# Second to fourth expert's down tiles freed singly, one load of each expert's count, and a first gather by token halves, in a one-core transformer layer

## The chip, the cores and the metric

The kernel is one layer of a diffusion backbone on one core of one Trainium2 chip. The metric is the device time of one execution in microseconds (us), the median of the runs shown. The core has a matrix engine (TensorE, PE), three engines for elementwise work (VectorE = DVE, ScalarE = ACT, GpSimd = POOL), and a sequencer without arithmetic (SyncE, SP) that issues here almost all transfers from memory (HBM) into the on-chip buffer (SBUF). PE writes to the accumulators (PSUM).

## The reference

For 256 latent tokens of width 1024 (plus 256 context tokens) the layer computes a mixer (gated linear attention and latent attention, merged and projected) and then a mixture of experts. Only the second part matters here:

```python
def _moe(h, p):
    tok = h.reshape(-1, d)
    logits = (tok @ p["router_w"] + p["router_b"]).astype(jnp.float32)
    top_v, top_i = lax.top_k(logits, TOP_K)          # 4 of 32
    wts = jax.nn.softmax(top_v, axis=-1)
    combine = jnp.sum(jax.nn.one_hot(top_i, N_EXPERTS) * wts[..., None], axis=1)
    out = jnp.zeros_like(tok)
    for e in range(N_EXPERTS):
        gate = jnp.minimum(tok @ p["w_gate"][e] + p["b_gate"][e], SWIGLU_LIMIT)
        up = jnp.clip(tok @ p["w_up"][e] + p["b_up"][e], -SWIGLU_LIMIT, SWIGLU_LIMIT)
        act = (up + 1.0) * gate * jax.nn.sigmoid(SWIGLU_ALPHA * gate)
        out = out + combine[:, e:e + 1] * (act @ p["w_down"][e] + p["b_down"][e])
    return out.reshape(b, t_len, d)
```

All weights are float32: 32 experts with three 1024 x 1024 matrices are 384 MiB, read once.

## The kernel before, in words

**Weights.** Each expert's three matrices come as six tiles of 2 MiB, in the order gate, gate, up, up, down, down (the last two experts have their downs at the very end). The tiles are called w0, w1, ... here, in the order of their issue: w0 to w5 are the first expert's, w6 to w11 the second's, and so on. `Ring` holds ten places: tile w(i) may be issued only when w(i-10) has been used and its place was given back with `ring.done` (line 92), which calls `pump`, whose transfers are issued on SP (L77). SP runs its list in order, so a transfer that waits for its place holds up everything behind it.

**One expert.** An expert has up to 64 token slots in the main path. The tokens of two experts at a time are gathered (`select` makes one-hot columns G on DVE from the position table `posm`, `gather` multiplies them with x1 on PE into `p_xg`, in two halves g of four 128-column blocks, and DVE and ACT scale the blocks into X). Then `project` for gate and up (PE, into `p_gate` and `p_up`), `gated` and `upped` (DVE, ACT), `turn` (four transposes on PE into `p_aT`, copied by ACT to aT), `down` (PE into `p_y`), `halves` (ACT, DVE), and `scatter`, which adds the result into the accumulators `acc`. The scatter of an expert is done in the next expert's turn. `slot_tokens` (PE `p_st`, then DVE) makes the slot-to-token table.

**Overflow.** An expert with more than 64 tokens has a second path inside `tc.If(rv > 0)`; rv is a register loaded from `trips` by `blocks(e)` (L1554), on every engine. In this run only the first expert of those looked at here takes that path; the others branch over it. A further block, `crowded()` (L1502, after the expert with index 20), is for still fuller experts and is branched over as well.

**When places are freed.** The first expert (index 0) and those with index 1 to 3 (`e < SINGLE`) give back each gate and up tile by itself with `freed(1)`; the first expert does so with its downs too, the next three give both downs back at once with `ring.done(2)` behind the whole down product. Experts with index 4 to 9 free in pairs. `freed` loads rv anew, ordered behind the transfer that it issued.

**Order on the engines.** In this part PE runs in the order in which the code is written (`manual_schedule` for PE). SP, DVE and ACT are ordered by the scheduler, so where register loads and branches stand on SP does not follow from the source alone.

**Before the experts.** The router's choice for the two halves of 128 tokens (`best`, `choose`), the positions (`p_pos`, `posm`), and the gather of the first two experts stand between the mixer and the first product. `more_gather` gathers the overflow tokens of the first expert; its `p_xg` takes a PSUM place of the same two-place tag as the main gather's.

Of the kernel before, what the change touches and what calls it, by code (L numbers as in the profile page):

```python
# [8 lines left out]
F32 = mybir.dt.float32  # L9
# [10 lines left out]
NE = 32  # L20
SLOTS = 64
# [108 lines left out]
def block_kernel(ctx: ExitStack, tc: tile.TileContext, a, out):  # L130
# [71 lines left out]
    def mm(o, l, r, start, stop):  # L202
        nc.tensor.matmul(o, l, r, start=start, stop=stop)  # L203
# [18 lines left out]
    def bank(name, shape=(128, 512)):  # L222
        return ps.tile(list(shape), F32, tag="b", bufs=3, name=name)
# [928 lines left out]
    def softmax(t, step):  # L1152

        v = sm[t]
        if step == 0:
            nc.vector.tensor_scalar(v[:, 4:5], mx[:, t, 0:1], -1.0, None, op0=ALU.mult)
            nc.scalar.activation(v[:, 0:4], mx[:, t, 0:4], AF.Exp, bias=v[:, 4:5], accum_out=v[:, 5:6])
        else:
            nc.vector.reciprocal(v[:, 6:7], v[:, 5:6])
            nc.vector.tensor_scalar(v[:, 0:4], v[:, 0:4], v[:, 6:7], None, op0=ALU.mult)  # L1160
            nc.vector.tensor_mul(eq[t], eq[t], v[:, 0:4].unsqueeze(1).to_broadcast([128, 32, 4]))
            nc.vector.tensor_reduce(comb[:, t], eq[t], axis=mybir.AxisListType.X, op=ALU.add)

# [67 lines left out]
    def best(t, p):  # L1231
        lg = lgs[t]
        nc.vector.scalar_tensor_tensor(lg, p, r2[t], rb, op0=ALU.mult, op1=ALU.add)
        nc.vector.max(mx[:, t], lg)
        nc.vector.max_index(ix[:, t], mx[:, t], lg)
        nc.vector.tensor_scalar(ixf[:, t], ix[:, t, :4], 1.0, None, op0=ALU.add)

    def choose(t):

        nc.vector.tensor_tensor(eq[t], iota[:, :32].unsqueeze(2).to_broadcast([128, 32, 4]),  # L1240
                                ixf[:, t].unsqueeze(1).to_broadcast([128, 32, 4]), op=ALU.is_equal)
        with nc.allow_low_precision(reason="0 or 1"):
            nc.vector.tensor_reduce(maskb[:, t], eq[t], axis=mybir.AxisListType.X, op=ALU.add)
# [5 lines left out]
    def warm(n):  # L1249

        for _ in range(n):
            mm(pw, zero.to_broadcast([128, 128]), zero.to_broadcast([128, 512]), True, True)
# [28 lines left out]
    p1 = logits(1)  # L1281
    choose(0)
    softmax(0, 0)
    best(1, p1)
    choose(1)
    softmax(1, 0)
    close(psz_cm)
    pa_cm, psa = pool("ps_acc", space=PSUM, reuse_waits="tile")
    acc = [[psa.tile([128, 512], F32, tag=f"acc{t}{n}", name=f"acc{t}{n}") for n in range(2)] for t in range(2)]
    for t in range(2):  # L1290
        for n in range(2):
            mm(acc[t][n], zero.to_broadcast([128, 128]), zero.to_broadcast([128, 512]), True, False)
    warm(4)
    p = bank("p_pos", (128, 3, 32))
    mm(p[:, 0], ltb, maskb[:, 0], True, True)
    mm(p[:, 1], ltb, maskb[:, 1], True, False)
    mm(p[:, 1], oneb, maskb[:, 0], False, True)
    mm(p[:, 2], oneb, maskb[:, 0], True, False)
    mm(p[:, 2], oneb, maskb[:, 1], False, True)
    nc.vector.scalar_tensor_tensor(posm, p[:, 0:2], 1.0, maskb, op0=ALU.add, op1=ALU.mult)  # L1300
    count = late.tile([1, 32], F32, name="count")
    trips = late.tile([1, 40], I32, name="trips")
    nc.scalar.copy(count, p[0:1, 2])

    close(ps_cm)
    pb_cm, psb = pool("ps_moe", space=PSUM, side="right", reuse_waits="tile")

    def bankb(name, shape=(128, 512), tag="b"):
        return psb.tile(list(shape), F32, tag=tag, bufs=2, name=name)

    close(op_cm)
    close(pre_cm)
# [11 lines left out]
    ring.pump()  # L1324
    loaded = ring.last

    def select(G, i, e):

        for t in range(2):
            nc.vector.tensor_scalar(G[:, t, i], iota[:, :SLOTS], posm[:, t, e:e + 1], r2[t], op0=ALU.is_equal, op1=ALU.mult)  # L1330

    def gather(X, G, g):

        p = bankb("p_xg", (128, 4, SLOTS * EB))
        for k in range(4):
            for t in range(2):
                mm(p[:, k], x1[:, t, ts(4 * g + k, 128)], G[:, t], t == 0, t == 1)
        for k in range(4):
            j = 4 * g + k
            if k % 2:  # L1340
                nc.scalar.activation(X[:, j], p[:, k], AF.Identity, bias=fB[:, 0, j:j + 1], scale=fA[:, 0, j:j + 1])
            else:
                nc.vector.tensor_scalar(X[:, j], p[:, k], fA[:, 0, j:j + 1], fB[:, 0, j:j + 1],  # L1343
                                        op0=ALU.mult, op1=ALU.add)
# [18 lines left out]
    def slot_tokens(of, sid, tag=""):  # L1363

        p = bankb("p_st")
        mm(p, of.to_broadcast([128, 128]), where, True, True)
        n = 1 if tag else 2
        S = mo.tile([128, 2, 128], F32R, tag="S" + tag, bufs=2, name="S")
        w = mo.tile([128, 1], F32, tag="wt" + tag, bufs=n, name="wt")
        hit = mo.tile([128, 256], BF16, tag="hit", name="hit")  # L1370
        s = S.rearrange("p a b -> p (a b)")
        nc.vector.tensor_scalar(s, p[:, :256], sid, None, op0=ALU.is_equal)
        nc.vector.scalar_tensor_tensor(hit, s.bitcast(F32), 1.0, p[:, 256:], op0=ALU.mult, op1=ALU.mult, accum_out=w)
        return S, w

    def block_tiles():
        return (mo.tile([128, 2, EB, SLOTS], F32, tag="G", name="G"),
                mo.tile([128, 8, EB * SLOTS], F32, tag="X", bufs=2, name="X"))
# [69 lines left out]
    def turn(u, slots, tag="", aT=None):  # L1448
        nt = slots // 16
        p = bankb("p_aT", (128, nt, 128), tag="b" if tag else "g")  # L1450
        for k in range(nt):
            nc.tensor.transpose(p[:, k], u[:, ts(k, 128)], C("ident"))  # L1452
        if aT is None:
            aT = mo.tile([128, nt, 128], F32, tag="aT" + tag, name="aT")
        nc.scalar.copy(aT, p)  # L1455
        return aT
# [24 lines left out]
    def scatter(S, ys):  # L1481

        for t in range(2):
            for y in ys:
                for h in range(2):
                    r = slice(SLOTS * h, SLOTS * h + SLOTS)
                    mm(acc[t][h], S[r, t], y[r], False, False)
# [41 lines left out]

    todo, gtf = None, bd  # L1530
    G, X = block_tiles()
    for i in range(EB):
        select(G, i, i)
    more = more_gather(SLOTS, posm[:, :, 0:1])
    next(more)
    gather(X, G, 0)
    gather(X, G, 1)
    next(more)
    next(more)

# [9 lines left out]
    def blocks(e, ins=None):  # L1550
        with ExitStack() as es:
            if ins is not None:
                es.enter_context(tc.issue_after(ins))
            return nc.values_load(trips[:1, e:e + 1], min_val=0, max_val=(256 - SLOTS) // MORE)  # L1554
# [10 lines left out]
            return Ws[4 + n][:, k]  # L1565
        return Ws[4 + k // 4][:, k % 4, ts(n, 512)]

    ends = {}
    for e in range(NE):
        i = e % EB  # L1570
        if e and i == 0:
            X = Xn
        Ws = [ring.take() for _ in range(6 if e < NE - 2 else 4)]

        def W(c, j):
# [8 lines left out]
        def freed(n):  # L1584

            ring.done(n)
            return blocks(e, ring.last.ins)

        if e == 0:

# [80 lines left out]
                else:  # L1671
                    ring.done(4)
        following = list(range(e - i + EB, e - i + 2 * EB))
        if following[0] < NE:
            if i == 0:
                Gn, Xn = block_tiles()
                for k, f in enumerate(following):
                    select(Gn, k, f)
                gather(Xn, Gn, 0)
            if i == 1:  # L1680
                gather(Xn, Gn, 1)
        aT = turn(u, SLOTS, aT=aT_last if e == NE - 1 else None)
        if e == NE - 1:
            pass
        elif e:
            scatter(*todo)
        if e + 1 < NE:
            toks[e + 1] = slot_tokens(sel[:, e + 1:e + 2], first_sid)
        if e == 24:

            cbT = mo.tile([128, 2, 128], F32, tag="aT1", name="cbT")
# [8 lines left out]
            row_all(gtf, 1, bankb)  # L1700
        S = toks.pop(e)[0]

        if e == 0:
            p = bankb("p_y", tag="g")
            ps_ = [bankb(f"p_y1{n}") for n in range(2)]
            for half in range(2):
                ks = range(4 * half, 4 * half + 4)
                down(aT, lambda k: Ws[4 + k // 4][:, k % 4], p, ks)
                if half:
                    todo = S, halves(p)  # L1710
                with tc.If(rv > 0):
                    if half == 0:
                        a1T = turn(u1, MORE, "1")
                    for n in range(2):
                        down_parts(a1T, lambda k: w_of(e, k, n), MORE, ps_[n], ks)
                    if half:
                        more_out(S1, ps_)
                rv = freed(1)
        elif e < NE - 2:
            todo = S, halves(down(aT, lambda k: Ws[4 + k // 4][:, k % 4], bankb("p_y", tag="g")))  # L1720
            with tc.If(rv > 0):  # L1721
                a1T = turn(u1, MORE, "1")
                more_out(S1, [down_parts(a1T, lambda k: w_of(e, k, n), MORE, bankb(f"p_y1{n}")) for n in range(2)])
            ring.done(2)
        else:
            ends[e] = S, S1, aT, u1, rv
# [181 lines left out]
```

## Time and profile before

| | |
|---|---|
| time, median of 3 runs (lowest, highest) | 1249.0 us (1248.04, 1249.89) |
| time of the profiled execution; its span | 1249.03 us; 1247.3 us |
| TensorE's granted clock, mean | 0.986 of full speed |
| PE busy, share of the span | 1147.7 us, 92% |
| DVE, ACT, POOL busy | 403.2, 243.9, 78.4 us |
| read from HBM | 460.53 MB, 370 GB/s over the span |

The span goes from the first to the last instruction in the trace. PE's busy share counts matmuls that are pipelined and whose ends are modelled, so 92% does not say that PE sets the time; the transfer rate by slices, below, has to be read beside it.

### The profile page before, as it was taken

The numbers are of one execution on the slowest core, as the hardware profiler recorded it, in microseconds if no ns is written. First come the engines' busy times: TensorE is split into PE (matmuls) and PEld (weight loads), VectorE is DVE, ScalarE is ACT, GpSimd is POOL, SyncE is SP. The second block draws the span as 40 slices with busy tenths as digits, with TensorE's granted clock in tenths as the row PEclk, the third lists the DMA queues.
The fourth block names the chain that finished last, engine by engine and source line by source line (L and its number), as shares of the span: only waits on it lengthen the run. The fifth ranks groups of instructions, "written<-read, shape, count | busy, mean of one in ns | idle before, by whom it ended". The sixth has DMA issues, their size and how long they took to land. (4 is left out here: it accounts for less than half of the span.)

```text
span 1247.3 us, 16381 instructions
## 1 busy us (share of the span) xinstructions
PE 1147.7 (92%) x6494; PEld 610.3 (49%) x6495; DVE 403.2 (32%) x780; ACT 243.9 (20%) x425; POOL 78.4 (6%) x61
## 2 busy tenths in 40 slices
PE   8999999999998999999999899999879989999886
PEld 5776699885333344444444344444334434444332
DVE  5667686675211212212121221222112211111112
ACT  4565544443200000101010010101000100101001
POOL 2355101300000000000000000000000000000000
PEclk9999999999999999999999999999989999999999
DMA  8933446986889999999999999999899999999995
GB/s 350 352 142 138 189 171 256 387 349 272 304 346 424 422 427 426 426 426 424 428 425 426 426 427 427 425 424 426 374 376 425 427 427 426 425 427 424 426 426 218
DMA packets 37190, 463.52 MB, mean 372 GB/s; under 512 B 4504, under 2 KB 4760, under 8 KB 9280
## 3 DMA queue, kind: packets, MB, share of 16 engines
q1 hardware_dynamic: 36336, 460.90, 88.7%
q8 instruction: 101, 1.65, 0.5%
q10 hardware_dynamic: 720, 0.70, 0.2%
q14 instruction: 33, 0.27, 0.1%
HBM read 460.53 MB, written 1.05 MB: 370 GB/s over the span
## 5 line engine op out<-in xcount | busy, mean ns | idle before, releaser
L203 PE MATMUL p_up<-w,X 128*64 128x512 f32 x1024 | 228.9, 594 | 10.5 <-DMA w<-in_w_up_dram 7.6
L203 PE MATMUL p_gate<-w,X 128*64 128x512 f32 x1024 | 229.9, 597 | 3.9 <-DMA w<-in_w_gate_dram 2.1
L203 PE MATMUL p_y<-w,aT 128*64 128x512 f32 (+1 forms) x1056 | 230.1, 601 | 1.8 <-ACT aT L1455 1.4
L203 PEld LDWEIGHTS p_up<-w,X 128*64 128x64 f32 x1024 | 91.4, 137 | 132.0 <-issue 113.5
L203 PEld LDWEIGHTS p_gate<-w,X 128*64 128x64 f32 x1024 | 94.1, 138 | 116.5 <-issue 113.5
L203 PEld LDWEIGHTS p_y<-w,aT 128*64 128x64 f32 (+1 forms) x1056 | 70.5, 136 | 141.6 <-issue 137.3
L1420 DVE TENSOR_SCALAR g<-p_gate 128x512 f32<-128x512 f32 x32 | 22.1, 692 | 221.8 <-PE p_gate L203 212.6
L203 PE MATMUL p_xg<-G,x 128*128 128x128 f32 x512 | 70.7, 295 | 24.3 <-PEq L1664 18.9
L1478 DVE TENSOR_TENSOR yl<-p_y,yh 128x512 fp32r<-128x512 f32 x31 | 21.4, 691 | 218.2 <-ACT yh L1477 209.2
L203 PEld LDWEIGHTS p_xg<-G,x 128*128 128x128 f32 x512 | 65.1, 206 | 49.3 <-issue 49.3
L1455 ACT COPY aT<-p_aT 128x512 f32<-128x512 f32 (+1 forms) x33 | 18.9, 574 | 309.8 <-PE p_aT L1452 309.8
L1425 DVE TENSOR_SCALAR u<-p_up 128x512 f32<-128x512 f32 x32 | 22.1, 691 | 170.6 <-PE p_up L203 170.6
L1421 ACT ACTIVATE s<-g 128x512 f32<-128x512 f32 (+1 forms) x34 | 21.0, 618 | 281.4 <-DVE g L1420 281.4
L1190 POOL TENSOR_TENSOR rx<-rx,cst 128x1 f32<-128x1 f32 x4 | 2.7, 674 | 992.3 <-DVE rx L1189 992.3
L1477 ACT CAST yh<-p_y 128x512 fp32r<-128x512 f32 x31 | 18.2, 586 | 205.9 <-PEq L1721 186.7
L203 PEld LDWEIGHTS <-selb 128*64 128x64 bf16 (+2 forms) x178 | 15.8, 104 | 80.7 <-issue 78.9
L1343 DVE TENSOR_SCALAR X<-p_xg,mA_gpref,mB_gpref 128x128 f32<-128x128 f32 x64 | 26.2, 409 | 69.2 <-PE p_xg L203 49.3
L203 PE MATMUL p_gate<-h0h,wsl 128*128 128x256 f32 x160 | 45.5, 284 | 2.5 <-DVE wsl L370 2.5
L203 PE MATMUL p_gate<-h0h,wsh 128*128 128x256 f32 x160 | 46.7, 292 | 0.0
L203 PE MATMUL p_gate<-h0l,wsh 128*128 128x256 f32 x160 | 44.9, 280 | 0.0
L370 DVE TENSOR_TENSOR wsl<-p,wsh 128x1024 fp32r<-128x1024 f32 x27 | 35.4, 1310 | 11.6 <-ACT wsh L369 11.5
L328 POOL TENSOR_TENSOR sums<-sums,f 128x1024 f32<-128x1024 f32 x14 | 35.8, 2590 | 33.5 <-ACT f L326 22.2
(422 smaller groups left out, 1392.6 us busy)
## 6 DMA issues: line engine op xcount, KB each, us to landing
w<-in_w_up_dram SPq DMA_DIRECT2D x64, 2048.0 KB, 31.2
w<-in_w_gate_dram SPq DMA_DIRECT2D x64, 2048.0 KB, 30.8
w<-in_w_down_dram SPq DMA_DIRECT2D x62, 2048.0 KB, 25.8
p<-in_w_in_dram SPq DMA_DIRECT2D x7, 2048.0 KB, 9.5
a<-in_w_mod_a_dram SPq DMA_DIRECT2D x8, 1024.0 KB, 9.6
f<-in_w_mod_f_dram SPq DMA_DIRECT2D x4, 2048.0 KB, 8.6
g<-in_w_mod_g_dram SPq DMA_DIRECT2D x4, 2048.0 KB, 8.4
wo<-in_w_out_dram SPq DMA_DIRECT2D x2, 2048.0 KB, 15.3
```

What stands on the lines that cost most here:

```text
L203: nc.tensor.matmul(o, l, r, start=start, stop=stop)
L328: nc.gpsimd.tensor_add(to, to, v)
L370: (eng or nc.vector).tensor_sub(lo, src, hi.bitcast(F32))
L1190: nc.gpsimd.tensor_tensor(dst, dst, C("nhalf")[:, :1], op=ALU.pow)
L1343: nc.vector.tensor_scalar(X[:, j], p[:, k], fA[:, 0, j:j + 1], fB[:, 0, j:j + 1], op0=ALU.mult, op1=ALU.add)
L1420: nc.vector.tensor_scalar(g, pg, LIMIT, None, op0=ALU.min)
L1421: nc.scalar.activation(s, g, AF.Sigmoid, scale=ALPHA)
L1425: nc.vector.tensor_scalar(u, pu, LIMIT, -LIMIT, op0=ALU.min, op1=ALU.max)
L1455: nc.scalar.copy(aT, p)
L1477: nc.scalar.copy(hi, p)
L1478: nc.vector.tensor_sub(lo, p, hi.bitcast(F32))
```

## The change: what it does

1. **Head.** The second half's choice (`best`, `choose`, `softmax` for tokens 128 to 255) is written behind the product that gives the first half's positions; `posm` is made for each half by itself. Six zero products (`warm`) stand between the two position products. The first gather runs by token halves: all eight blocks for the first 128 tokens, then all eight for the others, into two banks at once.
2. **First expert.** The gather of the next pair moves behind the downs; the next expert's `slot_tokens` ahead of the turn.
3. **Second to fourth expert** (index 1 to 3). The scatter of the expert before moves ahead of the turn, the gather behind the downs, and the downs are done and freed in two halves, each with its own `If`.
4. **Count.** `freed` returns the rv that the expert already has and loads nothing.

```diff
-    best(1, p1)
-    choose(1)
-    softmax(1, 0)
...
+    mm(p[:, 0], ltb, maskb[:, 0], True, True)
+    warm(6)
+    best(1, p1)
+    choose(1)
+    place_of(0)
+    softmax(1, 0)
+    mm(p[:, 1], oneb, maskb[:, 0], True, False)
+    mm(p[:, 1], ltb, maskb[:, 1], False, True)
...
+    pg = [bankb(f"p_xg{g}", (128, 4, SLOTS * EB)) for g in range(2)]
+    for t in range(2):
+        for i in range(EB):
+            select(G, i, i, [t])
+        if t == 0:
+            place_of(1)
+            nc.scalar.copy(count, p[0:1, 2])
+        for g in range(2):
+            for k in range(4):
+                mm(pg[g][:, k], x1[:, t, ts(4 * g + k, 128)], G[:, t], t == 0 and k == 0, t == 1 and k == 3)
...
             ring.done(n)
-            return blocks(e, ring.last.ins)
+            return rv
...
+        select_next()
+        if not single:
+            for_next()
         elif e:
             scatter(*todo)
-        if e + 1 < NE:
-            toks[e + 1] = slot_tokens(sel[:, e + 1:e + 2], first_sid)
+        else:
+            tokens_next()
+        aT = turn(u, SLOTS, aT=aT_last if e == NE - 1 else None)
+        if not single and e < NE - 1:
+            scatter(*todo)
+        if e:
+            tokens_next()
...
-        if e == 0:
+        if single:
             p = bankb("p_y", tag="g")
             ps_ = [bankb(f"p_y1{n}") for n in range(2)]
             for half in range(2):
...
                 rv = freed(1)
+            for_next()
```

`for_next` is the gather of the next pair, `tokens_next` is `slot_tokens` for the next expert.

**PE, second expert, from the end of its up product to the next expert.** w_2984 and w_3047 are its two down tiles (w10 and w11) in the kernel before. There it reads, without the rows inside the `If` that repeat:

```order
L1644 UNCONDITIONAL_BRANCH x2
L1554 TENSOR_LOAD trips
L203 MATMUL p_xg<-G,x_2294 128x128 x8
L1452 MATMUL p_aT<-cst,u 128x128 x4
L203 MATMUL acc_2811<-yh,S 128x512
...
L203 MATMUL p_st<-where,selb 128x512
L203 MATMUL p_y<-w_2984,aT 64x512 x8
L203 MATMUL p_y<-w_3047,aT 64x512 x8
L1721 COMPARE_AND_BRANCH
...
L1721 UNCONDITIONAL_BRANCH x2
```

In the changed kernel the same two tiles are w_2988 and w_3037:

```order
L1659 UNCONDITIONAL_BRANCH x2
L203 MATMUL acc_2803<-yh,S 128x512
...
L1458 MATMUL p_aT<-cst,u 128x128 x4
L203 LDWEIGHTS selb
L203 MATMUL p_st<-where,selb 128x512
L203 MATMUL p_y<-w_2988,aT 64x512 x8
L1740 COMPARE_AND_BRANCH
...
L203 MATMUL p_y<-w_3037,aT 64x512 x8
L1740 COMPARE_AND_BRANCH
...
L1740 UNCONDITIONAL_BRANCH x2
L203 MATMUL p_xg<-G,x_2294 128x128 x8
```

The register load and the gather are gone from in front of the transposes, the scatter stands there, the downs are parted by a branch, and the gather follows them.

**SP, around the branch over `crowded()`.** In the kernel before, w_8879 is w126 and w_8881 is w127; nothing stands between the end of that branch and w127:

```order
L77 DMA w_8877<-in_w_down_dram 128x4096
L77 DMA w_8879<-in_w_gate_dram 128x4096
L1721 COMPARE_AND_BRANCH
L1721 UNCONDITIONAL_BRANCH x2
L1502 COMPARE_AND_BRANCH
...
L1502 UNCONDITIONAL_BRANCH
L77 DMA w_8881<-in_w_gate_dram 128x4096
```

In the changed kernel w_8852 is w135 and w_9297 is w136. The pair of rows TENSOR_LOAD and ISA x2 of L1569 stands eleven times in a row, of which one is shown:

```order
L77 DMA w_8850<-in_w_up_dram 128x4096
L77 DMA w_8852<-in_w_up_dram 128x4096
L1758 TENSOR_LOAD trips
L1508 COMPARE_AND_BRANCH
...
L1508 UNCONDITIONAL_BRANCH
L1758 ISA x2
L1569 TENSOR_LOAD trips
L1569 ISA x2
...
L1679 COMPARE_AND_BRANCH
L1679 UNCONDITIONAL_BRANCH x2
L77 DMA w_9297<-in_w_down_dram 128x4096
```

The branch over `crowded()` has moved nine tiles further down SP's list, and the counts of the eleven experts that follow (index 21 to 31) are now loaded on SP between that branch and the next transfer. In the kernel before such bunches of loads (nine, twelve, twelve and three) stand ahead of w11, w20, w26 and w32.

**PE, ahead of the first expert.** p_xg is the gather; w_2199 is the first gate tile. Before, from the last position product on:

```order
L203 MATMUL p_pos<-maskb,oneb 128x32
L203 MATMUL p_xg<-G,x_2294 128x128 x16
L203 MATMUL p_xg<-x_2294,G 32x256 x8
L203 LDWEIGHTS selb
L203 MATMUL p_gate<-RB,selb 64x512
```

In the changed kernel p_xg_2868 and p_xg_2869 are the two banks of four blocks:

```order
L203 MATMUL p_pos<-maskb,oneb 128x32
L203 MATMUL p_xg_2868<-G,x_2294 128x128 x4
L203 MATMUL p_xg_2869<-G,x_2294 128x128 x4
L203 MATMUL p_xg_2868<-G,x_2294 128x128 x4
L203 MATMUL p_xg_2869<-G,x_2294 128x128 x4
```

The first bank is complete after three quarters of the products instead of after half of them.

## Rows read from the trace of the kernel before

**Rows 1.** The page: GB/s in 40 equal slices of the span (31.2 us each).

```profile
GB/s 350 352 142 138 189 171 256 387 349 272 304 346 424 422 427 426 426 426 424 428 425 426 426 427 427 425 424 426 374 376 425 427 427 426 425 427 424 426 426 218
```

**Rows 2.** Busy time by stretch: PE, PEld, DVE, ACT, POOL, clock, DMA share, GB/s.

```profile
345.00:375.00 30.00, 26.43 (x133) 11.21 (x133) 6.14 (x14) 2.62 (x5) 0.00 (x0) 1.00 0.86 342
435.00:1230.00 795.00, 730.12 (x3726) 326.07 (x3726) 159.92 (x335) 74.14 (x141) 0.00 (x0) 0.98 1.00 421
```

**Rows 3.** Timeline of SP: start, us, transfers of weight tiles issued (x2: two tiles).

```profile
345.45 4.54 SPq L77 DMA_DIRECT2D w<-in_w_down_dram  x2
354.04 4.54 SPq L77 DMA_DIRECT2D w<-in_w_gate_dram  x2
369.88 0.96 SPq L77 DMA_DIRECT2D w<-in_w_up_dram  x2
374.27 4.69 SPq L77 DMA_DIRECT2D w<-in_w_down_dram  x2
427.67 0.81 SPq L77 DMA_DIRECT2D w<-in_w_up_dram  x2
435.49 0.80 SPq L77 DMA_DIRECT2D w<-in_w_down_dram  x2
```

**Rows 4.** Weight tiles issued on SP at 369.9 us, then at 354.0: us to landing.

```profile
DMA to landing us min/median/max: 7.6/7.6/7.6
DMA to landing us min/median/max: 10.6/10.6/10.6
```

**Rows 5.** Timeline of PE, second expert: start, us, instruction, idle before and its end.

```profile
354.47 3.65 PE L203 MATMUL p_up<-w,X 128*64 128x512 f32 x16 [0.55 <-PEq L1644]
358.83 2.02 PE L203 MATMUL p_xg<-G,x 128*128 128x128 f32 x16 [0.70 <-PEq L1644]
360.69 0.60 PE L1452 MATMUL p_aT<-cst,u 128*128 128x128 f32 x4
362.66 7.09 PE L203 MATMUL p_y<-w,aT 128*64 128x512 f32 x32
370.28 0.44 PE L203 MATMUL p_gate<-RB,selb 128*64 128x512 bf16 x2 [0.53 <-PEq L1721]
```

**Rows 6.** Timeline of PE: the gather behind a branch, fifth expert and a later one.

```profile
443.90 2.02 PE L203 MATMUL p_xg<-G,x 128*128 128x128 f32 x16 [0.71 <-PEq L1664]
660.59 2.02 PE L203 MATMUL p_xg<-G,x 128*128 128x128 f32 x16 [0.30 <-PEq L1664]
```

**Rows 7.** Timeline of PE, first expert, from its up product to its downs.

```profile
324.07 2.05 PE L203 MATMUL p_xg<-G,x 128*128 128x128 f32 x16
325.96 0.60 PE L1452 MATMUL p_aT<-cst,u 128*128 128x128 f32 x4
327.23 3.65 PE L203 MATMUL p_y<-w,aT 128*64 128x512 f32 x16 [0.46 <-ACT aT L1455]
```

**Rows 8.** Timelines of PE and ACT ahead of the first expert's gate product.

```profile
293.81 3.81 PE L203 MATMUL p_xg<-G,x 128*128 128x128 f32 x32 [1.20 <-DVE G L1330]
297.76 1.07 PE L203 MATMUL p_xg<-x,G 128*32 128x256 f32 x16
298.76 0.41 PE L203 MATMUL p_gate<-RB,selb 128*64 128x512 bf16 x2
...
297.25 0.46 ACT L1341 ACTIVATE X<-p_xg,mB_gpref,mA_gpref 128x128 f32<-128x128 f32 x1 [0.48 <-DVE X L1343]
```

**Rows 9.** SP, the branch over `crowded()`: its waits, and the transfers around it.

```profile
L1502 SPq EVENT_SEMAPHORE  x9: 17/17/17, 869.2 to 906.6; - x9
DMA to landing us min/median/max: 38.4/38.4/38.4
868.13 38.91 SPq L77 DMA_DIRECT2D w<-in_w_gate_dram  x2
```

**Rows 10.** SP, one bunch of register loads between w19 and w20.

```profile
L1554 SPq TENSOR_LOAD <-trips x12: 262/263/278, 358.6 to 365.2; - x12
```

**Rows 11.** Timeline of PE: the first product behind the branch over `crowded()`.

```profile
917.61 0.67 PE L203 MATMUL p_gate<-RB,selb 128*64 128x512 bf16 x2 [7.50 <-PEq L1554]
```

More of the change, by code (lines that the diff above doesn't have):

```diff
@@ L1292, in block_kernel @@
             mm(acc[t][n], zero.to_broadcast([128, 128]), zero.to_broadcast([128, 512]), True, False)
[L1293 to L1303, printed above, removed]
     close(ps_cm)
@@ L1309, in bankb, with place_of @@
         return psb.tile(list(shape), F32, tag=tag, bufs=2, name=name)
+    def place_of(t):
+        nc.vector.scalar_tensor_tensor(posm[:, t], p[:, t], 1.0, maskb[:, t], op0=ALU.add, op1=ALU.mult)
+    p = bankb("p_pos", (128, 3, 32), "g")
+    pw = bankb("p_warm", tag="g")
+    mm(p[:, 0], ltb, maskb[:, 0], True, True)
[6 more added lines that the diff above has]
+    mm(p[:, 1], ltb, maskb[:, 1], False, True)
+    mm(p[:, 2], oneb, maskb[:, 0], True, False)
+    mm(p[:, 2], oneb, maskb[:, 1], False, True)
+    count = late.tile([1, 32], F32, name="count")
+    trips = late.tile([1, 40], I32, name="trips")
     close(op_cm)
@@ L1325, in block_kernel, with select @@
     loaded = ring.last
-    def select(G, i, e):
-        for t in range(2):
+    def select(G, i, e, ts_=range(2)):
+        for t in ts_:
             nc.vector.tensor_scalar(G[:, t, i], iota[:, :SLOTS], posm[:, t, e:e + 1], r2[t], op0=ALU.is_equal, op1=ALU.mult)
@@ L1337, in gather, with gathered @@
                 mm(p[:, k], x1[:, t, ts(4 * g + k, 128)], G[:, t], t == 0, t == 1)
+        gathered(X, p, g)
+    def gathered(X, p, g):
         for k in range(4):
@@ L1531, in block_kernel @@
     G, X = block_tiles()
-    for i in range(EB):
-        select(G, i, i)
+    pg = [bankb(f"p_xg{g}", (128, 4, SLOTS * EB)) for g in range(2)]
[8 more added lines that the diff above has]
+                mm(pg[g][:, k], x1[:, t, ts(4 * g + k, 128)], G[:, t], t == 0 and k == 0, t == 1 and k == 3)
     more = more_gather(SLOTS, posm[:, :, 0:1])
     next(more)
-    gather(X, G, 0)
-    gather(X, G, 1)
+    for g in range(2):
+        gathered(X, pg[g], g)
     next(more)
@@ L1566, in w_of @@
         return Ws[4 + k // 4][:, k % 4, ts(n, 512)]
-    ends = {}
+    ends, ahead_of = {}, []
     for e in range(NE):
@@ L1571, in block_kernel @@
         if e and i == 0:
-            X = Xn
+            X = ahead_of[1]
         Ws = [ring.take() for _ in range(6 if e < NE - 2 else 4)]
@@ L1673, in block_kernel, with select_next, for_next, tokens_next @@
         following = list(range(e - i + EB, e - i + 2 * EB))
-        if following[0] < NE:
-            if i == 0:
-                Gn, Xn = block_tiles()
+        single = e < SINGLE
+        def select_next():
+            if following[0] < NE and i == 0:
+                ahead_of[:] = block_tiles()
                 for k, f in enumerate(following):
[L1678 to L1684, printed above, removed]
+                    select(ahead_of[0], k, f)
+        def for_next():
+            if following[0] < NE:
+                gather(ahead_of[1], ahead_of[0], i)
+        def tokens_next():
+            if e + 1 < NE:
+                toks[e + 1] = slot_tokens(sel[:, e + 1:e + 2], first_sid)
+        select_next()
+        if not single:
+            for_next()
         elif e:
             scatter(*todo)
-        if e + 1 < NE:
-            toks[e + 1] = slot_tokens(sel[:, e + 1:e + 2], first_sid)
+        else:
[5 more added lines that the diff above has]
+            tokens_next()
         if e == 24:
```

## The prediction

> **What bounds the kernel now.** PE's busy share of 92% suggests PE, so I read the transfer rate by slices first [rows 1]: from the thirteenth slice (some 375 us) to the last but one it stands at 422 to 428 GB/s, with a dip at the twenty-ninth and thirtieth. By windows [rows 2] the DMA engines are busy 0.86 of 345 to 375 us, but 1.00 of 435 to 1230. So in the long part the transfers set the time, and PE has to wait now and then. A tile of 2 MiB (2.097 MB) at 426 GB/s takes 4.9 us. What counts is therefore when the unbroken stream begins, and where it breaks off later.
>
> When it begins is read from SP's timeline [rows 3]. If all later tiles follow at 4.9 us each, tile w(i), issued at t, sets an end of t − 4.9 i plus a constant. I call t − 4.9 i its lateness; the largest one holds the chain. With the issue times of [rows 3]: w16 345.45 − 78.4 = 267.1; **w20 369.88 − 98.0 = 271.9**; w32 427.67 − 156.8 = 270.9; w34 435.49 − 166.6 = 268.9. w20 holds it. It was issued into an empty queue: it landed after 7.6 us, where w18 (issued 354.0) took 10.6 [rows 4]. And w20 is the tile that takes the place of w10, the second expert's first down tile, given back with w11 behind the whole down product: 362.66 + 7.09 = 369.75 on PE [rows 5], issue at 369.88. The change frees that place earlier.
>
> Where it breaks is seen at the branch over `crowded()` on SP [rows 9]. SP has issued w126 in the pair at 868.13, then stands in nine waits until 906.6. Those waits are for transfers already issued: w126 needs 38.4 us to land, that is until 906.5, and w127 is issued only behind it: the pair's row ends at 868.13 + 38.91 = 907.04, w127's being the last part of it. So the queue is emptied. A lone tile lands 7.6 us after its issue [rows 4] where 4.9 is the rhythm; with the step from 906.5 to an issue at some 906.7 this is a hole of about 7.8 − 4.9 = 2.9 us, and the stream never gets it back.
>
> **The change, part by part.**
>
> *Head.* Before, the gather's 32 products take 3.81 us from 293.81, with 1.20 us of waiting for G ahead of them; the overflow gather follows at 297.76, when ACT is done with the bank's place (297.25 + 0.46 = 297.71), and the first gate product at 298.76 [rows 8]. Now the first bank is complete after 24 products instead of 16, a quarter of 3.81 or 0.95 us later, and its four blocks are scaled later. Against that, the first half of the products need not wait for the second half's positions, which can save part of the 1.20; I take about half, 0.55. Sum +0.4 us (bounds: +0.95 with nothing saved; −0.7 if all 1.20 is saved and the scaling hides half of the 0.95 too). The zero products lie in front of that, while PE waits for `choose`, and cost nothing; if they were in the way, nothing of the 1.20 would be saved, which is the +0.95.
>
> *First expert.* The gather (324.07 to 325.96, 1.89 us) moves behind the downs, and `p_st` no longer covers the copy of aT, where PE waits already 0.46 [rows 7]. The gather's time is the same at either place, so +0.3 us for the copy (0 to 0.4, one p_st). The second expert starts 0.4 + 0.3 = 0.7 us later, and w16, which waits for that expert's first gate tile, is issued at 345.45 + 0.65 = 346.1: lateness 267.7.
>
> *Register loads.* The gap behind a branch with a load is 0.71 us, without one 0.30 [rows 6]; the smaller gap of 0.55 [rows 5] leaves 0.25. I take 0.3 each. The second expert loses three ahead of its last up product's end or at it: −0.9 on the way.
>
> *Second expert's downs.* Before, from the end of up (354.47 + 3.65 = 358.12) to the downs (362.66) it is 4.54 us. The gather goes out (360.69 − 358.83 = 1.87), the load behind the branch too (0.41 by [rows 6]), and the scatter now stands ahead of the turn, so that only `p_st` covers the copy of aT: +0.46 as in [rows 7]. That is 2.73. The downs start at 358.12 + 0.65 − 0.9 + 2.73 = 360.6, and half of them end at 360.6 + 3.55 = 364.2. w20 is issued at about 364.3, lateness 266.3. One more branch (0.30) and the gather behind the downs put the next expert's first gate product where it was (364.2 + 3.55 + 0.3 + 1.87 + 0.3 = 370.2, before 370.28), so w22 and w23 stay (374.1, before 374.27). The third and fourth expert win about the same 0.9 each (loads −1.4, branch +0.3, copy +0.4, and small change): w32 falls below 268, w34 comes at 433.4, lateness 266.9. The largest lateness is then w16's 267.7.
>
> *What the stream wins.* 271.9 − 267.7 = 4.1 us at most. But around w16 the queue is thin, and then tiles do not land at 4.9: w16 alone would land at 345.45 + 7.6 = 353.05 and w18 at 362.85, yet w18 landed at 354.04 + 10.6 = 364.64, 1.8 us later. A part of this stays, since w17 to w19 still come one by one; I take 1.1, a little above the middle of 0 and 1.8. Early gain: **3.0 us** (bounds 1.8 with all of it and the head at +0.95, to 4.8 with none of it and the head at −0.7).
>
> *What moves on SP.* The loads dropped from `freed` free SP of bunches that lay in front of tiles where SP had to wait for a place anyway, such as twelve ahead of w20 [rows 10]: no gain there. But the order shows eleven loads (experts 21 to 31) behind the branch over `crowded()`, ahead of w136, and the branch now behind w135. It still waits until what is issued has landed. Behind it SP executes eleven loads before it may issue anything, with the queue empty. [rows 10] gives the price: twelve loads start from 358.6 to 365.2, eleven steps, 0.60 us each with the register instructions between them. 11 × 0.60 = 6.5 us (bounds 4.7, if a load costs only what a branch gap lost, 0.41 to 0.43, and 6.9). What is queued behind them is w136 and every later tile, and PE waits for those, having no other tile left. The hole grows from 2.9 to 9.4 us. No tile lands meanwhile and PE does not set the pace afterwards, so all of it is lost: **+6.5 us**.
>
> *The rest.* Experts 4 to 9 lose two loads each (0.3 to 0.4, some 0.7 an expert) on PE, in the stretch where the DMA share is 1.00 [rows 2]: nothing. If the cover were gone it would be −4 us.
>
> **Sum**, against the profiled execution's own 1249.03, which is the median (1249.0): 1249.03 − 3.0 + 6.5 = **1252.5 us**. Bounds: 1249.03 − 4.8 + 4.7 = 1248.9, and 1249.03 − 1.8 + 6.9 = 1254.1.
>
> **Rivals.**
> 1. *The loads at the drain cost nothing at the end* (other side). If SP gets at the loads while transfers are still on the way, or the end is set by PE rather than by the stream, the hole stays at 2.9. For it: loads hid elsewhere. Against it: order on SP, nine waits in front, a share of 1.00. Then 1249.0 − 3.0 = 1246.0 (1244.2 to 1247.2). It brings the time below that of before if less than 3.0 of the 6.5 us is exposed, and below it by over 0.2% if less than 0.5 is.
> 2. *The early gain does not come.* The stream begins as late as before, because w17 to w19 hold it, or the head costs 3 us more. For it: 1.8 us were lost there. Against: the lateness of w20 falls by 5.6. Time 1249.0 + 6.5 = 1255.5.
> 3. [...] The first product behind PE's branch over `crowded()` waits 7.50 us, with no tile to blame [rows 11]; the ordinary branches cost 0.30 [rows 6]. Three new branches, one in each expert's downs, could cost 7 us each: w34 would come 2 × 7 to 3 × 7 later than 433.4, about 450, lateness 283, 12 over w20's 271.9 of before; with the drain, 1249.0 + 12 + 6.5 = 1267. Against it: they skip blocks as short as those already skipped at 0.30.
>
> [...]
>
> **How the numbers follow.** Forecast 0.76, rival 1 0.12, rival 2 0.08, rival 3 0.04. 0.2% is 2.5 us, about what a measurement of this kernel can tell from no change: faster means below 1246.5, slower above 1251.5. Of the forecast's 1248.9 to 1254.1 I put 0.56 above 1251.5 and 0.20 within. Rival 1 gives 0.10 faster and 0.02 the same; rivals 2 and 3 are slower. Faster 0.10, same 0.22, slower 0.68. The range 1248.0 to 1255.6 takes in the forecast's bounds and rival 2, and leaves out rivals 1 and 3, 0.16. The likeliest case's own range is 1248.9 to 1254.1.
>
> **What would show it.** Early: the first gate product at about 299.1; w16 issued near 346.1 and w20 near 364.3 instead of 369.88; a gap near 0.3 behind the branch ahead of the second expert's scatter; w34 about 2 us earlier. Late: on SP nine waits behind w135, then eleven loads over 6.5 us with the DMA queue empty, w136 landing some 14 us after w135. If w136 lands 8 us behind w135, rival 1 holds. If w34 is later than 435.5, rival 2 or 3. Wrong, too, if the last tile's landing moves and the end does not follow it.

## The result and the profile after

The changed kernel takes 1255.04 us (median of 5 runs, 1254.32 to 1257.94), the kernel before 1249.0 (1247.27 to 1250.61): ratio 1.0056, 95% interval 1.0045 to 1.0066. It is slower, by 6 us in the medians and 7 by the ratio, where 3.5 were forecast. The direction was right; of the two terms of the sum one was right to 0.3 us, and the other did not come at all.

First the page's transfer rate by slices, which answers to [rows 1]:

```profile
GB/s 348 349 125 152 176 170 256 390 346 274 277 374 428 425 424 427 426 425 425 427 425 426 426 428 420 427 425 427 425 424 227 427 426 427 426 425 426 426 425 230
```

The dip to 374 and 376 in the twenty-ninth and thirtieth slice is gone, and the thirty-first stands at 227: one deeper hole, one or two slices later. Windows around it (columns as in [rows 2]):

```profile
435.00:915.00 480.00, 445.50 (x2378) 200.36 (x2374) 101.06 (x215) 45.85 (x88) 0.00 (x0) 1.00 1.01 426
915.00:960.00 45.00, 36.56 (x174) 16.04 (x172) 7.52 (x16) 3.26 (x7) 0.00 (x0) 0.89 0.72 304
960.00:970.00 10.00, 8.18 (x48) 4.53 (x45) 2.13 (x3) 0.58 (x1) 0.00 (x0) 1.00 0.86 342
970.00:1230.00 260.00, 231.94 (x1126) 99.18 (x1125) 48.73 (x100) 23.95 (x45) 0.00 (x0) 0.99 1.01 426
```

To both sides of the hole the stream runs without a break, at 426 GB/s. So the kernel's time is still made of two things: when the stream begins, and what the hole takes.

**The hole.** SP's instructions behind w135, from the views of single lines: the waits of the branch over `crowded()`, then the loads of the counts, each with two register instructions. The columns are duration in ns (minimum, median, maximum) and the first and last start in us; "..." marks rows left out.

```profile
L1508 SPq EVENT_SEMAPHORE  x9: 17/17/17, 917.3 to 953.7; - x9
...
L1569 SPq TENSOR_LOAD <-trips x11: 263/263/271, 954.0 to 959.6; - x11
L1569 SPq FUSED_REGOPS  x11: 147/147/152, 954.3 to 960.0; - x11
L1569 SPq SEQ_ASSERT  x11: 18/18/18, 954.5 to 960.1; - x11
```

And SP's timeline there:

```profile
916.09 0.38 SPq L77 DMA_DIRECT2D w<-in_w_up_dram  x1
960.45 0.81 SPq L77 DMA_DIRECT2D w<-in_w_down_dram  x2
```

The last wait ends at 953.7 (w135, issued at 916.1, landed after 37.1 us), eleven loads run from 954.0 to 960.1, and w136 is issued at 960.45. That is 6.7 us from the last wait to the issue, where [rows 9] had 906.6 to 906.7 for w127. The forecast's 6.5 us is there, instruction for instruction.

**The beginning.** The profiled execution (1257.43) reaches the first weight tile 2.14 us later than that of before: w0 is issued at 196.95 instead of 194.81. The instructions up to there are the same in both kernels; the last section shows where the time goes. (w0 is the first weight tile that is issued; in both traces it is one of the up matrix.) So early times below are given from w0's issue: "net" means less 2.14, that is, on the clock of the kernel before. PE's timeline of the first expert, which answers to [rows 7] and the head in [rows 8]:

```profile
301.21 0.41 PE L203 MATMUL p_gate<-RB,selb 128*64 128x512 bf16 x2
...
324.16 1.93 PE L203 MATMUL p_m<-w,X 128*32 128x256 f32 x32
326.02 0.39 PE L203 MATMUL p_st<-where,selb 128*128 128x512 bf16 x1
328.78 0.63 PE L1458 MATMUL p_aT<-cst,u 128*128 128x128 f32 x4 [2.37 <-DVE u L1432]
330.08 5.35 PE L203 MATMUL p_y<-w,aT 128*64 128x512 f32 x16 [0.67 <-ACT aT L1461]
```

The first gate product starts at 301.21, net 299.07; forecast 299.1. But then PE waits 2.37 us for u, and the first half of the downs runs 5.35 us instead of 3.65. DVE's timeline there says why u is late:

```profile
326.16 0.42 DVE L1431 TENSOR_SCALAR u<-p_m 128x256 f32<-128x256 f32 x1 [6.71 <-PE p_m L203]
326.62 0.42 DVE L1432 SCALAR_TENSOR_TENSOR u<-u,g 128x256 f32<-128x256 f32 x1
326.96 0.68 DVE L1431 TENSOR_SCALAR u<-p_up 128x512 f32<-128x512 f32 x1
...
327.95 0.68 DVE L1432 SCALAR_TENSOR_TENSOR u<-u,g 128x512 f32<-128x512 f32 x1
```

DVE makes the overflow's u (128x256) first and the main u (128x512) behind it, although the main `p_up` is complete when `p_m`, the overflow's product, starts at 324.16. It idles 6.71 us for `p_m`. In the kernel before it is the other way round:

```profile
322.32 0.69 DVE L1425 TENSOR_SCALAR u<-p_up 128x512 f32<-128x512 f32 x1 [5.28 <-PE p_up L203]
323.05 0.69 DVE L1426 SCALAR_TENSOR_TENSOR u<-u,g 128x512 f32<-128x512 f32 x1
324.21 0.42 DVE L1425 TENSOR_SCALAR u<-p_m 128x256 f32<-128x256 f32 x1 [0.47 <-PE p_m L203]
```

There DVE's load of the count starts at 323.06 and the branch of the overflow path at 323.44, both behind the start of the main u. In the changed kernel the branch has no load in front of it, and the scheduler has put it ahead of the main u, as DVE's order shows:

```order
L1636 COMPARE_AND_BRANCH
L1431 TENSOR_SCALAR u1_3112<-p_m1_3051 128x256
L1432 SCALAR_TENSOR_TENSOR u1_3112<-u1_3112,g1_3032 128x256
L1636 UNCONDITIONAL_BRANCH
L1636 UNCONDITIONAL_BRANCH
L1431 TENSOR_SCALAR u_2923<-p_up_3050 128x512
```

What became of it on SP, which answers to [rows 3]:

```profile
351.77 4.13 SPq L77 DMA_DIRECT2D w<-in_w_down_dram  x2
359.56 4.13 SPq L77 DMA_DIRECT2D w<-in_w_gate_dram  x2
369.99 4.13 SPq L77 DMA_DIRECT2D w<-in_w_up_dram  x2
```

Net, w16 comes at 349.63, lateness 271.2, w20 at 367.85, lateness 269.9. So w16 holds the chain, as forecast, but at 271.2 and not at 267.7: only 0.7 less than w20's 271.9 before. w34 is issued at 439.74, net 437.6, lateness 271.0, nearly as late; 433.4 was forecast. From w0's issue to the landing of w36 it is 460.00 − 196.95 = 263.05 us, before 457.58 − 194.81 = 262.77. The early gain is nil (−0.3).

### The profile page after: what moved, and what is told of

It reads as the page before. It is cut to its first block, busy times and chain, and to the rows that moved or that the text cites. A ratio compares the mean times of both kernels' runs of the same rounds, so it can differ in the third digit from the quotient of the medians.

```text
span 1255.7 us, 16172 instructions
## 1 busy us (share of the span) xinstructions
PE 1146.1 (91%) x6494; PEld 604.0 (48%) x6497; DVE 405.0 (32%) x781; ACT 244.3 (19%) x425; POOL 78.3 (6%) x61
## 5 line engine op out<-in xcount | busy, mean ns | idle before, releaser
L203 PEld LDWEIGHTS p_up<-w,X 128*64 128x64 f32 x1024 | 88.8, 137 | 134.7 <-issue 115.1
L203 PE MATMUL p_xg<-G,x 128*128 128x128 f32 x512 | 67.7, 288 | 30.6 <-PEq L1679 20.8
L203 PEld LDWEIGHTS p_xg<-G,x 128*128 128x128 f32 x512 | 62.5, 199 | 55.2 <-issue 50.2
L203 PEld LDWEIGHTS <-selb 128*64 128x64 bf16 (+2 forms) x178 | 14.7, 104 | 72.4 <-issue 69.6
```

## The experiments

One number sums up a trace: the time from w0's issue to the landing of the last piece of the last down, since the same work lies in front of it and behind it. Before 1234.04 − 194.81 = 1039.2 us, after 1243.27 − 196.95 = 1046.3. I call it the stream's length. Ratios are to the kernel before, run beside each group. 0.1% is 1.25 us.

**e1, the counts spread.**

```diff
-        rv = blocks(e) if e else None
+        rv = blocks(e, ring.last.ins) if e else None
```

> The changed kernel, but each expert's count is loaded behind the transfer issued last, one load at a time, so that no bunch of eleven stands behind the drain on SP (the branch over crowded() now stands behind w132, and w133 directly behind it). Theory A (the eleven loads hold the empty queue for 6.5 us): the hole is 2.9 us again, time 1255.0 - 6.5 = 1248.5 us. Rival C (the drain itself got dearer, because it stands some tiles further on): the time stays at 1255. In both the first expert keeps PE's wait of some 2.4 us for u.

Ratio 1.0007 (0.9998 to 1.0016), 1249.01 us; length 1040.4. SP's timeline at the drain, and the first tile behind it:

```profile
901.03 35.92 SPq L77 DMA_DIRECT2D w<-in_w_gate_dram  x2
937.06 0.84 SPq L77 DMA_DIRECT2D w<-in_w_up_dram  x2
...
DMA to landing us min/median/max: 7.6/7.6/7.6
```

The waits end at 936.5, w133 is issued at 936.6 and lands 7.6 us later. The hole is the old one: w132 to w134 take 13.9 us by landings where two tiles take 9.8, that is 4.1, beside 4.3 in the kernel before and 11.0 in the changed one. 6.1 us are back (1.0056 − 1.0007 = 0.0049). Rival C is out: where the drain stands is not what it costs.

**e2, the first expert loads its count anew.**

```diff
             ring.done(n)
-            return rv
+            return rv if e else blocks(e, ring.last.ins)
```

> The changed kernel, but the first expert alone loads its count anew after each freed tile. On DVE its main u then stands ahead of the overflow's u again; the eleven loads behind the drain stay. Theory A (the early gain is lost because DVE makes the overflow's u first, PE waits 2.4 us and the next product runs 1.7 us longer at a lower granted clock): 1255.0 - 3.5 = 1251.5 us, wait ahead of the first transposes under 1 us. Rival B (the early gain is lost because the gather left its place ahead of the transposes, whatever DVE's order): wait stays near 2.4 us, time 1255.

Ratio 1.0022 (1.0013 to 1.0031), 1250.28 us; length 1042.2. DVE's and PE's timelines:

```profile
321.59 0.69 DVE L1431 TENSOR_SCALAR u<-p_up 128x512 f32<-128x512 f32 x1 [5.13 <-PE p_up L203]
322.31 0.69 DVE L1432 SCALAR_TENSOR_TENSOR u<-u,g 128x512 f32<-128x512 f32 x1
323.47 0.42 DVE L1431 TENSOR_SCALAR u<-p_m 128x256 f32<-128x256 f32 x1 [0.47 <-PE p_m L203]
```

```profile
323.56 0.60 PE L1458 MATMUL p_aT<-cst,u 128*128 128x128 f32 x4
324.84 3.65 PE L203 MATMUL p_y<-w,aT 128*64 128x512 f32 x16 [0.68 <-ACT aT L1461]
```

The main u is first again, PE waits for no u, the product takes 3.65 us, and w16 is issued at 344.83 (w0 at 193.87). Theory A's 1251.5 is met (1.0022 × 1249.0 = 1251.7), rival B's 1255 is not. The second expert answers to [rows 5]:

```profile
356.46 0.50 PE L203 MATMUL acc<-yh,S 64*128 64x512 f32 x2
...
357.91 0.63 PE L1458 MATMUL p_aT<-cst,u 128*128 128x128 f32 x4 [0.25 <-DVE u L1432]
...
359.27 3.65 PE L203 MATMUL p_y<-w,aT 128*64 128x512 f32 x16 [0.52 <-ACTq L1740]
363.09 3.66 PE L203 MATMUL p_y<-w,aT 128*64 128x512 f32 x16 [0.16 <-PEq L1740]
367.04 2.02 PE L203 MATMUL p_xg<-G,x 128*128 128x128 f32 x16 [0.30 <-PEq L1740]
369.00 0.41 PE L203 MATMUL p_gate<-RB,selb 128*64 128x512 bf16 x2
```

w20 is issued at 363.06. With w0 0.94 earlier than before, that is 364.0 on the clock of [rows 3], where the forecast had 364.3. The two branches cost 0.16 and 0.30: rival 3 of the prediction is out.

**e3, both edits.** The diffs of e1 and e2 together.

> Both edits of the two runs before at once. Theory A: 1255.0 - 6.5 - 3.5 = 1245.0 us, faster than the kernel before by some 4 us. Rival B: 1248.5. Rival C: 1251.5.

Ratio 0.9977 (0.9967 to 0.9987), 1244.91 us; length 1036.3. The two costs are separate and add up: 0.0049 and 0.0034 taken off 1.0056 give 0.9973. Cured of both, the change wins 2.9 us: the forecast's early gain of 3.0.

**e4, the count edit alone, in the kernel before.**

```diff
             ring.done(n)
-            return blocks(e, ring.last.ins)
+            return rv
```

> The kernel before with the count edit alone (freed gives back the rv it has). SP then has the eleven loads behind the drain ahead of w136, and DVE the overflow's u ahead of the main u in the first expert, as in the changed kernel. Theory A: 1249.0 + 6.5 for the hole, + 2 for the wait for u that the gather does not cover wholly, - 0.9 for the loads left out: some 1256.5 us (1255 to 1259). Rival B: no wait in the first expert, 1249.0 + 6.5 - 0.9 = 1254.6. Rival C: 1249.

Ratio 1.0044 (1.0031 to 1.0058), 1253.77 us; length 1043.9. The hole is there: w136 is issued at 956.99. But the first expert hardly suffers:

```profile
323.51 2.05 PE L203 MATMUL p_xg<-G,x 128*128 128x128 f32 x16
326.00 0.63 PE L1452 MATMUL p_aT<-cst,u 128*128 128x128 f32 x4 [0.44 <-DVE u L1426]
327.31 3.65 PE L203 MATMUL p_y<-w,aT 128*64 128x512 f32 x16 [0.67 <-ACT aT L1455]
```

DVE makes the overflow's u first here too, and yet PE waits only 0.44 us: the gather, still ahead of the transposes, fills the time. My expectation (+2) was wrong: the time is rival B's (1.0044 × 1249.0 = 1254.5, rival B 1254.6), and rival B had half of the truth. The run also shows what the dropped loads win by themselves: w36 lands 260.9 us after w0's issue, 1.9 less than before, and the larger hole stands against that. Theory A, that the order on DVE alone loses the early gain, becomes theory A': it takes the late u and the gather's departure together.

**e5, `crowded()` late.** The kernel of e3 with

```diff
-        if e == 20:
+        if e == 29:
```

> The kernel of e3 (loads spread, the first expert's count loaded anew), with the branch over crowded() behind the expert with index 29 instead of 20, so that SP's drain stands ahead of w187, eleven transfers before the end. If the drain costs 2.9 us wherever the stream is still running: no change against e3 (ratio 0.9977, 1244.9 us at 1247.5 for before). If its price is that a lone tile lands in 7.6 instead of 4.9 us, and this hides nothing at the end either, the same. Only if PE has work of its own left at the end, under which the hole fits, it falls to some 1242 us (ratio 0.9955). I expect 1245.

Ratio 0.9986 (0.9977 to 0.9995), 1246.99 us: not better than e3. The stream's length is 1035.4, 0.9 shorter, but the last landing at 1228.7 is followed by 17.7 us to the end of the span (1246.4), against 14.4 in e3 (1229.6 to 1244.0): PE is behind when the data are there. A later drain buys nothing.

**e6, the first expert's old order.** The kernel of e3 with

```diff
-        if not single:
+        if not single or not e:
             for_next()
         elif e:
             scatter(*todo)
-        else:
-            tokens_next()
...
-        if e:
-            tokens_next()
+        tokens_next()
...
-            for_next()
+            if e:
+                for_next()
```

> The kernel of e3 with the first expert in its old order (the gather of the next pair ahead of the transposes, the slot table behind them). Theory A (the order of the first expert alone costs next to nothing once DVE makes the main u first; forecast +0.3 us for it): 1244.6 us, not to be told from e3. Rival B (moving the gather is what loses the early gain): 1241.5.

Ratio 0.9961 (0.9948 to 0.9975), 1243.91 us; length 1034.9. w16 follows w0 by 150.8 us (345.97 − 195.19), in e3 by 150.9: +0.1 for the first expert's new order, as small as priced. The ratio alone would not decide: its interval overlaps e3's, and rival B's 1241.5 (0.9951) lies in it too. The issue of w16 does, and so does the landing of w36, 258.98 us after w0's issue and 259.22 in e3.

**e7, the old head.** The kernel of e3 with the head's lines of before (both choices first, one `posm`, the gather by banks): the minus lines of the diff above in place of its plus lines.

> The kernel of e3 with the head as before (both choices first, one posm, the gather by banks). The forecast priced the new head at +0.4 us (-0.7 to +0.95): 1244.5 us, not to be told from e3. The first gate product then starts about 0.4 us earlier, counted from the issue of w0.

Ratio 0.9963 (0.9949 to 0.9976), 1243.71 us; length 1036.2. From the start of the last `p_lg` product (the router's) to the first gate product it is 297.08 − 286.90 = 10.18 us, in e3 297.56 − 287.06 = 10.50: the new head costs 0.32 us. Forecast +0.4. The lengths agree, and the ratios' intervals overlap.

**e8, the old downs.** The kernel of e3 with the second to fourth expert's part undone, that is, the downs freed together and the orders around them as before:

```diff
-        single = e < SINGLE
+        single = e < 1

         def select_next():
```

> The kernel of e3 with the second to fourth expert as before behind up (gather, transposes, scatter, both downs freed together). If the downs freed singly carry the early gain of e2 and e3, w20 is issued some 5 us later, counted from w0, and the time is 1244.9 + 3 = 1248 us (ratio near 1.000). If the gain comes from anything else, it stays at 1245.

Ratio 0.9996 (0.9987 to 1.0005), 1247.05 us; length 1038.2. Without this part, which the change was most about, 1.9 (by length) to 2.4 us (by ratio) of e3's gain go. w20 is issued at 367.03, w0 at 193.33, so 173.7 us apart, in e3 169.2 (362.44 − 193.29).

**e9, gather ahead and u late.** The edits of e1 and e6, no load in `freed`.

> The kernel of e1 (loads spread, DVE still makes the overflow's u first) with the first expert in its old order, the gather ahead of the transposes. It completes the square of e1, e3 and e6 (gather ahead or behind, main u first or last). Theory A' (it takes both: the gather covers the late u): PE waits for u only some 0.4 us, as in e4, ratio about 0.996 to 0.997, some 1243.5 us at 1247.6 for before. Theory A as first stated (the order on DVE alone loses the gain): as e1, 1249.

Ratio 0.9978 (0.9969 to 0.9987), 1245.71 us; length 1035.9; the wait for u is 0.44 us, as in e4:

```profile
325.60 0.63 PE L1458 MATMUL p_aT<-cst,u 128*128 128x128 f32 x4 [0.44 <-DVE u L1432]
326.91 3.65 PE L203 MATMUL p_y<-w,aT 128*64 128x512 f32 x16 [0.46 <-ACT aT L1461]
```

The square of lengths is closed: gather ahead 1034.9 with the main u first and 1035.9 with it last; gather behind 1036.3 and 1040.4. Either step alone costs 1.0 to 1.4 us, both cost 5.5. In the first expert itself the steps cost less: w36 lands 258.98 and 259.60 us after w0's issue, then 259.22 and 264.19, so 0.2 and 0.6 alone and 5.2 together; the rest arises later in the stream, and its cause is open. Theory A' holds by either count.

**e10, zero products in the wait.** The kernel of e1 with, ahead of `turn`,

```diff
+        if e == 0:
+            pw2 = bankb("p_warm2")
+            for _ in range(9):
+                mm(pw2, zero.to_broadcast([128, 128]), zero.to_broadcast([128, 512]), True, True)
```

> The kernel of e1 with nine zero products of 512 columns on PE in front of the first expert's transposes, where PE waits 2.4 us for u. They change no data. If the first down product runs 5.4 to 6.1 us instead of 3.65 because PE stood idle and the granted clock fell, it takes 3.65 again and the time is 1249.0 - 2 = 1247 us; the waits for u and aT together stay. If the product is long for another reason, 1249.

Ratio 0.9989 (0.9980 to 0.9998), 1247.31 us; length 1037.8, 2.6 less than e1. Windows of e1, then of e10, which show the granted clock in the column behind the POOL's:

```profile
324.00:326.00 2.00, 0.36 (x2) 0.39 (x3) 1.83 (x5) 0.00 (x0) 0.00 (x0) 0.86 0.94 315
326.00:328.00 2.00, 1.32 (x6) 0.62 (x6) 0.00 (x0) 0.58 (x1) 0.00 (x0) 0.50 1.03 434
328.00:330.00 2.00, 2.00 (x6) 0.47 (x4) 0.00 (x0) 0.00 (x0) 0.00 (x0) 0.50 0.72 303
330.00:332.00 2.00, 2.00 (x8) 0.70 (x6) 0.00 (x0) 0.00 (x0) 0.00 (x0) 0.50 0.06 25
```

```profile
324.00:326.00 2.00, 1.60 (x10) 0.72 (x7) 1.75 (x5) 0.00 (x0) 0.00 (x0) 1.00 1.03 340
326.00:328.00 2.00, 1.33 (x8) 0.48 (x8) 0.00 (x0) 0.58 (x1) 0.00 (x0) 1.00 1.02 426
```

In e1 PE is busy 0.36 of 2 us, the granted clock falls to 0.50 and stays there over the downs: 6.05 us for a product of 3.65. With the zeros it stays at 1.00, and the product takes 3.65. w16 follows w0 by 150.9 us in e3, 153.2 here and 156.0 in e1: of the 5.1 us that the late u cost in e1, 2.3 are the wait and 2.8 the clock behind it.

**e11, both old orders.** The kernel of e6 with the head of e7: what is left is the second to fourth expert's part and the count loaded once, spread (the first expert's anew).

> The kernel of e6 with the head as before too: what remains of the change is the second to fourth expert's downs freed singly with the orders around them, and one load of each count behind the transfer issued last. By the forecast's terms: e6 (ratio 0.9961) less 0.3 for the head, ratio 0.9958, some 1242.5 us at 1247.6 for before.

Ratio 0.9965 (0.9952 to 0.9979), 1244.42 us; length 1034.9. Not to be told from e6 and e7. These three are 0.35 to 0.39% below the kernel before and 0.9% below the changed one.

## Why the prediction was right and wrong

*What bounds the kernel.* Right. Stream and hole account for the runs: what the length differs by from 1039.2 meets the ratio, taken as time, to 0.8 us in every run but e5 (2.0 us slower, for its end) and e7 (1.6 faster, with the length of e3; no trace says why).

*The eleven loads behind the drain, +6.5 us.* Right: 6.7 us from the last wait to the issue, 6.1 us in e1 against the changed kernel; in e4 the same larger hole stands against the 1.9 us that the dropped loads win early, which leaves its 5.5 by ratio, 4.7 by length. (11 × 0.60 is 6.6, not 6.5.) Rival 1, that they cost nothing, is out. What it had wrong there is smaller: by landings w135 to w138 take 25.71 us where three tiles take 14.7, so the whole hole is 11.0 and not 9.4; but that of before is 4.3 by the same count (w126 to w127 7.80, w127 to w130 16.14), not 2.9. Tiles behind the first one after the drain are late too (in e1 w134 lands 6.0 us behind w133, where the rhythm is 4.9), which the forecast left out of both holes, so their difference, 6.7, stood. The trace has no landing of w136 and w137, so the forecast's "some 14 us" for w136 can't be read.

*The early gain, −3.0 us.* This is the step that failed, at "*First expert*": "+0.3 us for the copy (0 to 0.4, one p_st)". I counted the gather's time, the same at either place, and the copy of aT, and took it that u is there when the transposes come, because it was there before. I read the order on SP and PE and not on DVE, where the dropped load had let the overflow's branch go ahead of the main u. The gather would have covered the late u (e4, e9: 0.44 us of waiting), and with the main u first no cover is needed (e2, e3: no wait for u). The change did both steps at once, and the forecast had neither as a term. Put right: a wait of 2.37 us, a product 1.70 longer at a lower clock (0.72 of full speed as a mean of 330 to 336 us, 1.00 from 318 to 326), w16 3.5 later than the forecast's 346.1. Put into the prediction's own rule this gives a lateness of 271.2, a gain of 0.7, and 1249.0 − 0.7 + 6.5 = 1254.8, beside 1255.04. That it comes so near is in part luck: the rule's deduction of 1.1 for the thin queue is left out of it, by landings the gain is −0.3 and the hole 6.7, and the lengths' +7.1 fits the ratio (1256.0). With the late u cured, the forecast's places are met: in e3 w16, w20 and w34 come, counted as net, at 345.7, 364.0 and 433.7 (forecast 346.1, 364.3, 433.4). In numbers the result is the prediction's second rival, "The early gain does not come" (1255.5, chance 0.08), and the sign named for it, w34 later than 435.5, is there (net 437.6). Neither of the reasons named there holds: the stream was late because w16 was, ahead of w17 to w19, and the head cost 0.32 us. The upper bound of 4.8 for this gain does not come out of its terms either: 4.1 and 1.1 for the head are 5.2.

*The other terms.* The head +0.4: measured +0.32. The second expert's gap in front of the scatter: about 0.3 expected; PE's scatter starts at 363.39 in the changed kernel, 0.16 behind the last up product (359.58 + 3.65). The downs freed singly: e8 puts 1.9 to 2.4 us on them with the orders around them, the largest part of the 3.0; e4 puts up to 1.9 on the dropped loads. The branches in the downs: 0.16 to 0.30.

The third rival's 7 us for each new branch was an estimate from the one stall at `crowded()` [rows 11]; none of the new branches showed one (in e2 0.16 and 0.30 us). PE's branch over `crowded()` still stalls, 7.60 us in the changed kernel (915.5 to 923.1, 6.30 of it the compare-and-branch itself), while SP waits for the queue to empty (to 953.7); what takes the time on PE there, no run shows.

## What to carry to other kernels

A register load or a wait that is taken away also takes away an order: where a scheduler places instructions, look at every engine's list behind the edit, above all at branches that can now go ahead of the main path, and at loads that now gather behind a drain. A step moved off an engine's path takes its cover along: before pricing the move, write down what other engines did meanwhile, and whether the next step needs it. And look at the granted clock behind a wait on PE: in e1 it fell to 0.50, and of the 5.1 us lost 2.8 were the clock's and 2.3 the wait's.

## What the runs showed of the hardware

*The wait and the clock.* In e1 PE waited 2.37 us for u (busy 0.36 of the 2 us from 324), and the granted clock stood at 0.50 from 326 to 332 us. In the changed kernel, behind the same wait of 2.37 us, it was 0.75 from 330 to 332 us and 0.50 from 332 to 334, and the next product took 1.70 us longer. In e10 nine zero products (2.13 us) filled the wait, and the clock was 1.00 in every window from 322 to 336.

*A shift that is not the change's.* Of the 2.14 us by which the profiled execution of the changed kernel is late at w0, 1.8 arise between 71 and 77 us, in the mixer. DVE and POOL in the trace of the changed kernel:

```profile
71.06 2.73 DVE L800 TENSOR_SCALAR pe<-pe,mx 128x512 f32<-128x512 f32 x1
...
74.49 2.60 DVE L370 TENSOR_TENSOR wsl<-p,wsh 128x1024 fp32r<-128x1024 f32 x1
```

```profile
68.77 10.58 POOL L328 TENSOR_TENSOR sums<-sums,f 128x1024 f32<-128x1024 f32 x4 [11.32 <-issue]
```

The same two instructions took 0.49 and 1.47 us in the trace of before, and there the first takes long at other places (1.91 us at 77.65, 2.57 at 124.39). Each time POOL is at work beside DVE for a part of it at least, but it is so beside short ones too (in the trace of before, two of the first kind at 0.49 us and nine of the second at 1.21 to 1.23). That the two contend was not tested. It fits that the changed kernel's five runs lie in two groups, 1254.3 to 1255.0 and 1257.4 to 1257.9, and that runs of the kernel before spread over 2.4 to 3.3 us in their groups; only the profiled ones can be looked into, so this stays a guess. From w0 on the issues of w1 to w9 agree to 0.2 us in all thirteen traces, which is why lengths counted from there tell more than one run's time.
